# Where the scaled down-projection weights and a residual correction stand in GpSimd's queue

## The chip, the cores and the metric

The kernel runs on one core of a Trainium2 chip. The core has five engines that run side by side, each with its own queue that is worked off in order: PE (TensorE, matrix products), DVE (VectorE), ACT (ScalarE), POOL (GpSimd) and SP (SyncE, which here only issues DMA transfers). They wait for one another through semaphores. The metric is the device time of one execution in microseconds (us), taken as the median of several runs; lower is better. One of those executions is recorded by the hardware profiler, and all durations below are from that record.

## What is computed

One decoder block on a 1024 x 1024 float32 activation: a state-space branch and an attention branch, merged by gates, and a feed-forward network. The change lies in the feed-forward network, of which the reference says:

```python
h = modulate(rmsnorm(x, norm2_g[l]), sh2, sc2)
ffn = (jax.nn.silu(h @ w_ffn_gate[l]) * (h @ w_ffn_up[l])) @ w_ffn_down[l]
x = x + g2 * ffn
...
return rmsnorm(x, norm_f_g)
```

`h` is 1024 x 1024, the hidden width is 2816, and `g2` is a row of 1024 gates. The kernel multiplies the rows of `w_ffn_down` by `g2` instead of the product, so the down projection adds straight to the residual `x`.

## The kernel before

**Pairs.** The hidden width is cut into 11 pieces of 256 columns, called pairs. Piece 10 is computed plainly. Pairs 0 to 9 go through `gate_up`, one after the other, each as a block scheme of seven products for gate and up instead of eight (`ORDER` gives the order of the seven). For every one of the seven, `operand` (L462) forms a weight block: where two blocks have to be added, POOL adds them into a staging tile (L471); ACT makes the rounded high part (L473), DVE the low part (L474). Each product is three matmuls per slice (high by high, high by low, low by high), 12 matmuls for gate and 12 for up, into one PSUM bank each. There are 8 banks, so the fifth product of a pair can only start when the banks of the first are free again.

**Emptying the banks.** `combine` (L1280) adds the seven products into four tiles `f1`: the first product is copied by ACT (L1284), the third too (L1288), the others are added by DVE (L1286 to L1299). Pool `F` holds four buffers of `f1`, all of which a pair uses, so a pair's first copy L1284 has to wait until a buffer of the pair before is free.

**End of a pair.** ACT applies silu to the two gate tiles (L1261), DVE multiplies by up (L1262), and POOL forms five sums of quarters (L1268), called *the pair's sums* below: three into new places, two in place. Then SP issues four DMA writes of the four tiles to `hD` in device memory (L1271). Only when these writes have landed are the `f1` buffers free for the next pair's L1284 and L1288.

**Rows of the down projection.** The down projection runs in three steps (`STEPS` = 4, 3 and 3 pairs), again as seven products. For the first step the right-hand operands are prepared beside `gate_up`: a row block `ft` of `w_ffn_down` is loaded by SP (L1194), multiplied by `g2` on POOL (L1195, *scaling*), and every second pair `down_sums` takes two scaled blocks, lets SP write two quarters to `hD` as they are (L1306), forms five quarter sums on POOL (L1311) in three groups that share one tile `gf`, and has each group written to `hD` (L1313). `ft` has two buffers, `gf` one.

**Start of the down projection.** `down` loads the residual into `acc`, scales the weights of the later steps on POOL (L1340), and corrects one quarter of the residual by two others with four POOL operations on 128 x 1024 (L1363, *the correction*). Its operand tiles partly live in the same `f1` buffers.

**What sets the order.** In this part no order is written by hand. A planner simulates the engines and puts each instruction in its engine's queue, the earliest in the program first among those that are ready in its simulation. `after(ins, first)` (L502) adds an edge that only orders: `ins` is placed behind `first` by the planner, and where the two are on different engines the chip waits for nothing on that account. Once placed, the queues are fixed; on the chip an instruction that is not ready holds up everything behind it on its engine.

Of the kernel before, what the change touches and what calls it, by code (L numbers as in the profile page):

```python
# [9 lines left out]
F32 = mybir.dt.float32  # L10
# [3 lines left out]
ALU = mybir.AluOpType  # L14
# [346 lines left out]
P = 128  # L361
# [25 lines left out]
SIGN_B = {i: ALU.subtract if i in (3, 4) else ALU.add for i in range(1, 8)}  # L387
# [38 lines left out]
class Block:  # L426
# [754 lines left out]
    def ffn(self, const, tp):  # L1181
        nc, i = self.nc, self.i
        wv = [i[n][0].rearrange("(k p) n -> p k n", p=P) for n in ("w_ffn_gate", "w_ffn_up")]
        w_v = i["w_ffn_down"][0].rearrange("(m p) n -> m p n", p=P)
        rows = []
        self.plain(10, wv)
        for j in range(10):
            self.gate_up(j, wv, tp)
            if j == 0:
                g2 = self.rp.tile([P, 1024], F32, name="row")  # L1190
                self.ada_row(g2, 6, tp, self.banks, ("ft", None))
            elif j <= 2 * STEPS[0]:
                rows.append(tp.tile([P, 1024], F32, name="ft"))
                nc.sync.dma_start(out=rows[-1], in_=w_v[j - 1])  # L1194
                nc.gpsimd.tensor_tensor(rows[-1], rows[-1], g2, ALU.mult)  # L1195
                if j % 2 == 0:
                    self.down_sums(j // 2 - 1, rows[-2:], tp)
        self.exp_ln(*self.silus)
        self.down(const, tp, g2)

# [33 lines left out]
    def gate_up(self, pair, wv, tp):  # L1234

        nc = self.nc
        A = {}
        for x, y in ((1, 0), (1, 1), (0, 0), (0, 1)):
            t = A[x, y] = self.W.tile([P, 2, 4, P], F32, name="wb")
            for q in range(2):  # L1240
                nc.sync.dma_start(out=t[:, q], in_=wv[q][:, 4 * y:4 * y + 4, 256 * pair + P * x:256 * pair + P * x + P])
        C = [[self.F.tile([P, 1024], F32, name="f1") for _ in range(2)] for _ in range(2)]
        M = [{}, {}]
        flat = lambda t: t.rearrange("p q k n -> p (q k n)")
        for n, i in enumerate(ORDER):
            if i not in self.B:
                b11, b12, b21, b22 = self.blocks
                u, v, pool, tag = {4: (b21, b11, self.PA, "pa"), 3: (b12, b22, self.PB, "pb"), 1: (b11, b22, self.X, "x1"),
                                   6: (b11, b12, self.X, "x1"), 7: (b21, b22, self.F, "f0")}[i]
                self.B[i] = self.pieces(i, u, v, pool, tag, Turns((tp, "ft")))  # L1250
            a, b = TERMS_A[i]
            w = self.operand(flat(A[a]), b and flat(A[b]), SIGN_A[i], None, *(nc.vector if pair == 0 or (i, e) in AENG else nc.gpsimd for e in range(2)))
            w = [t.rearrange("p (q k n) -> p q k n", q=2, k=4) for t in w]
            for q in range(2):
                ps = M[q][i] = self.banks.tile([P, 512], F32)
                self.seven(ps, w, q, i)
                self.combine(i, M[q], [C[q][0][:, 0:512], C[q][0][:, 512:1024], C[q][1][:, 0:512], C[q][1][:, 512:1024]])
        self.silus = []
        for x in range(2):
            g, u = C[0][x], C[1][x]  # L1260
            self.silus.append(nc.scalar.activation(g, g, AF.Silu))  # L1261
            nc.vector.tensor_tensor(u, u, g, ALU.mult)  # L1262
        L, R = slice(0, 512), slice(512, 1024)
        (g0, g1), (u0, u1) = C
        a11, a12, a21, a22 = u0[:, L], u1[:, L], u0[:, R], u1[:, R]
        for o, a, b, op in ((g0[:, L], a11, a22, ALU.add), (g0[:, R], a21, a22, ALU.add), (g1[:, L], a11, a12, ALU.add),
                                           (a21, a21, a11, ALU.subtract), (a12, a12, a22, ALU.subtract)):
            nc.gpsimd.tensor_tensor(o, a, b, op)  # L1268
        for n, t in ((0, u0), (2, u1), (4, g0), (6, g1[:, L])):
            w = t.shape[-1] // 512  # L1270
            nc.sync.dma_start(out=self.hD[pair, :, n:n + w, 0], in_=t.rearrange("p (a b) -> p a b", a=w))  # L1271
# [26 lines left out]
        elif i == 7:  # L1298
            tt(c[0], m[7], c[0], ALU.add)  # L1299

    def down_sums(self, pair, rows, tp):

        nc = self.nc
        part = lambda ax: rows[ax[0]][:, 512 * ax[1]:512 * ax[1] + 512]
        for i in (2, 5):
            nc.sync.dma_start(out=self.hD[pair, :, SLOT[i], 1], in_=part(TERMS_B[i][0]))  # L1306
        for group in ((3, 6), (7, 4), (1,)):
            t = tp.tile([P, 2, 512], F32, name="gf", bufs=1)
            for n, i in enumerate(group):
                a, b = TERMS_B[i]  # L1310
                nc.gpsimd.tensor_tensor(t[:, n], part(a), part(b), SIGN_B[i])  # L1311
            s = SLOT[group[0]]
            nc.sync.dma_start(out=self.hD[pair, :, s:s + len(group), 1], in_=t[:, 0:len(group)])  # L1313

    def down(self, const, tp, g2):
# [36 lines left out]
        for s, np_ in enumerate(STEPS):  # L1352
            W = [(weights(2 * p), weights(2 * p + 1)) if s else None for p in range(p0, p0 + np_)]
            if s == 1:
                gf = tp.tile([P, 1024], F32, name="gf", bufs=1)
                nc.scalar.dma_start(out=gf, in_=self.i["norm_f_g"].partition_broadcast(P))
            if s == len(STEPS) - 1:
                WL = [weights(20 + m) for m in range(2)]
            for n, i in enumerate(ORDER if s else FIRST):
                if s == 0 and n == 2:  # L1360
                    for z, op in ((5, ALU.add), (4, ALU.subtract)):
                        for a in range(2):
                            nc.gpsimd.tensor_tensor(flat(acc[7][a]), flat(acc[7][a]), flat(acc[z][a]), op)  # L1363
                ops = []
                (ay, ax), b = TERMS_B[i]
                for p in range(np_):
                    st = stages.tile([P, 1024], F32)
                    h, l = tiles()
                    if s == 0:
                        nc.sync.dma_start(out=st.rearrange("p (a b) -> p a b", a=2), in_=self.hD[p, :, SLOT[i]])  # L1370
                        self.operand(st, tiles=(h, l))
                        ops.append((h, l))
                        continue
                    nc.sync.dma_start(out=st[:, L], in_=self.hD[p0 + p, :, SLOT[i], 0])
                    u = W[p][ay][:, 512 * ax:512 * ax + 512]
                    if b is None:
                        for q, v in ((L, st[:, L]), (R, u)):
                            nc.scalar.copy(h[:, q], v)
                            nc.vector.tensor_tensor(l[:, q], v, h[:, q].bitcast(F32), ALU.subtract)
                    else:  # L1380
                        last_sum = nc.gpsimd.tensor_tensor(st[:, R], u, W[p][b[0]][:, 512 * b[1]:512 * b[1] + 512], SIGN_B[i])  # L1381
                        nc.scalar.copy(h, st)
                        nc.vector.tensor_tensor(l, st, h.bitcast(F32), ALU.subtract)
                    ops.append((h, l))
                if s == len(STEPS) - 1:
                    if n == 6:
                        rest = []
                        for m in range(2):
                            st = self.W.tile([P, 1024], F32, name="wb", bufs=4)
                            nc.sync.dma_start(out=st, in_=self.lD[m])  # L1390
                            rest.append((self.operand(st, tiles=tiles()), self.operand(WL[m], tiles=tiles())))
                    closing(n)
                for t in range(4):
                    ps = self.banks.tile([P, 512], F32)
                    j = 0
                    for o in ops:
                        for x, y in PRODUCTS:
                            nc.tensor.matmul(ps, lhsT=o[x][:, P * t:P * t + P], rhs=o[y][:, R], start=(j == 0), stop=(j == 3 * np_ - 1))  # L1398
                            j += 1
                    m = {z: acc[z][t // 2][:, t % 2] for z in acc}  # L1400
                    if s == 0 and i not in FROM:
                        (nc.scalar.copy if (n * 4 + t) % 2 else nc.vector.tensor_copy)(m[i], ps)
                    else:
                        nc.vector.tensor_tensor(m[i], ps, m[i], ALU.add)
            p0 += np_
# [176 lines left out]
```

## Time and profile before

| | us |
|---|---|
| median of 3 runs | 1488.67 |
| lowest and highest | 1486.19, 1491.62 |
| the profiled execution, its own time | 1486.86 |
| its span, first to last instruction | 1485.1 |

The span holds the input projection, the two branches and the output projection up to some 819 us, piece 10 and pairs 0 to 9 from there to 1250 us, and then the down projection with the last norm. In the timelines below a row gives start, duration, engine, line, operation, destination and sources, how many were merged, and in brackets how long the engine had been idle before and what ended that.

### The profile page before, as it was taken

To read this page: it belongs to the slowest core of one execution; us is meant where nothing else is said; L and a number is where in the kernel's file an instruction comes from. 1 tells how busy PE (TensorE), PEld (TensorE's weight loads), DVE (VectorE), ACT (ScalarE), POOL (GpSimd) and SP (SyncE) were. 2 spreads that over 40 slices of the span, in tenths; PEclk is the share of its full clock that TensorE was granted. 3 is DMA by queue.
4 is the path that set the end of the run, shared out by engine and by line. 5 is a ranking of instruction groups with operands and counts; after the bars stand their busy time and mean duration, and the time that the engine had idled before them with its cause. 6 is when DMAs were issued, how large, how long until landed. Compare 5 with 4: busy or idle time off the path is not lost.

```text
span 1485.1 us, 18288 instructions
## 1 busy us (share of the span) xinstructions
PE 1417.7 (95%) x6730; PEld 1121.3 (76%) x6730; DVE 1100.0 (74%) x1436; ACT 633.9 (43%) x859; POOL 497.4 (33%) x265
## 2 busy tenths in 40 slices
PE   5898999999999999999999999898999999999996
PEld 3678888787666666658887788787888888788884
DVE  5779996357797989877715598776756667879997
ACT  3321122632587767773339343222323334443425
POOL 1000000101211112104300017888644449328796
PEclk9999999999999999999999999999999999999998
DMA  9555665479111012126533134545433339745312
GB/s 341 136 112 166 159 166 133 148 251 353 35 50 50 29 43 78 51 76 236 180 118 128 43 86 149 186 164 181 150 101 99 104 105 359 240 130 175 100 57 114
DMA packets 186042, 207.19 MB, mean 140 GB/s; under 512 B 28892, under 2 KB 128288, under 8 KB 185952
## 3 DMA queue, kind: packets, MB, share of 16 engines
q1 hardware_dynamic: 176816, 198.49, 41.9%
q10 hardware_dynamic: 8912, 7.48, 1.8%
q8 instruction: 53, 0.87, 0.2%
q14 instruction: 37, 0.30, 0.1%
q0 software_dynamic: 224, 0.05, 0.0%
HBM read 148.69 MB, written 56.10 MB: 138 GB/s over the span
## 4 chain that ended last, share of the span: by engine, by line
PE 61%; DVE 14%; issue 7%; DMA 6%; POOL 6%; ACT 5%; SPq 0%; DVEq 0%; POOLq 0%; ACTq 0%
PE tq L1277 10%; PE mx L812 5%; PE mm L1277 5%; PE wo L1277 5%; PE ga L738 4%; PE mm L812 4%; PE mm L738 3%; PE acc L812 2%; PE mm L1117 2%; PE mm L646 2%; PE mx L738 2%; PE z L812 2%; PE wo L1117 2%; PE tq L1226 2%; PE tq L1117 1%
## 5 line engine op out<-in xcount | busy, mean ns | idle before, releaser
L471 POOL TENSOR_TENSOR ws<-wb 128x1024 f32<-128x1024 f32 x24 | 61.6, 2567 | 184.2 <-DVE wl L474 162.1
L455 POOL TENSOR_TENSOR wl<-ws,wh 128x1024 fp32r<-128x1024 f32 x12 | 30.7, 2562 | 162.7 <-ACT wh L452 99.3
L905 DVE TENSOR_TENSOR wa<-wa,acc 128x512 f32<-128x512 f32 (+1 forms) x80 | 47.0, 628 | 32.6 <-ACT row L903 30.2
L294 POOL MEMSET tz<- 128x1024 f32 x4 | 3.8, 954 | 178.0 <-PE mm L646 96.0
L877 ACT ACTIVATE ws<-wa 128x1024 f32<-128x1024 f32 (+1 forms) x40 | 39.1, 976 | 48.5 <-DVE wa L874 48.2
L1268 POOL TENSOR_TENSOR f<-f,f 128x512 f32<-128x512 f32 x30 | 53.2, 1800 | 16.0 <-DVE f L1262 10.7
L882 DVE TENSOR_TENSOR wl<-ws,wh 128x1024 fp32r<-128x1024 f32 (+1 forms) x40 | 57.1, 1427 | 1.0
L982 DVE SCALAR_TENSOR_TENSOR acc<-aw,cond,acc 128x512 f32<-128x512 f32 x56 | 46.0, 821 | 6.8 <-DMA aw<-in_w_ada_dram 6.1
L1261 ACT ACTIVATE f<-f 128x1024 f32<-128x1024 f32 x20 | 21.2, 1062 | 67.4 <-DVE f L1297 39.6
L474 DVE TENSOR_TENSOR wl<-ws,wh 128x1024 fp32r<-128x1024 f32 x20 | 33.7, 1683 | 19.7 <-ACT wh L473 19.6
L880 DVE SCALAR_TENSOR_TENSOR ws<-wa,ws 128x1024 f32<-128x1024 f32 (+1 forms) x40 | 45.5, 1137 | 3.0 <-ACT ws L879 2.0
L1398 PE MATMUL tq<-f,f 128*128 128x512 f32 x156 | 47.2, 389 | 0.0
L908 ACT ACTIVATE wa<-wa 128x1024 f32<-128x1024 f32 (+1 forms) x40 | 38.8, 971 | 19.5 <-DVE wa L905 18.5
L452 ACT CAST wh<-ws 128x1024 fp32r<-128x1024 f32 x24 | 25.1, 1049 | 49.8 <-PE wo L1117 23.3
L812 PE MATMUL z<-q,k 64*128 64x512 f32 (+3 forms) x192 | 41.8, 526 | 3.6 <-DVE wa L874 2.4
L471 POOL TENSOR_TENSOR wgs<-wb 128x1024 f32<-128x1024 f32 x12 | 30.8, 2570 | 41.2 <-DVE wgl L474 14.9
L1277 PE MATMUL tq<-x,wh 128*128 128x512 f32 x144 | 44.3, 389 | 0.0
L1277 PE MATMUL tq<-pa,wh 128*128 128x512 f32 x144 | 44.3, 389 | 0.0
L1340 POOL TENSOR_TENSOR pa<-pa,row 128x1024 f32<-128x1024 f32 x14 | 42.0, 3038 | 0.0
L454 POOL TENSOR_SCALAR wh<-ws 128x1024 fp32r<-128x1024 f32 x6 | 7.7, 1277 | 102.3 <-issue 36.1
L1381 POOL TENSOR_TENSOR wb<-pa 128x512 f32<-128x512 f32 x14 | 23.1, 1655 | 55.9 <-DVE wl L474 37.9
L812 PE MATMUL mm<-wa,V 128*64 128x512 f32 (+3 forms) x192 | 39.8, 507 | 0.0
(948 smaller groups left out, 4751.8 us busy)
## 6 DMA issues: line engine op xcount, KB each, us to landing
aw<-in_w_ada_dram SPq DMA_DIRECT2D x64, 256.0 KB, 4.5
hD<-f SPq DMA_DIRECT2D x30, 512.0 KB, 4.0
ws<-in_w_in_dram SPq DMA_DIRECT2D x23, 512.0 KB, 4.3
wb<-in_w_ffn_gate_dram SPq DMA_DIRECT2D x44, 256.0 KB, 4.0
wb<-in_w_ffn_up_dram SPq DMA_DIRECT2D x44, 256.0 KB, 4.5
x<-in_x_dram SPq DMA_DIRECT2D x16, 512.0 KB, 7.1
pb<-in_w_ada_dram SPq DMA_DIRECT2D x16, 512.0 KB, 9.4
gD<-gst SPq DMA_DIRECT2D x32, 256.0 KB, 2.1
```

The source lines that it names most:

```text
L471: (add or nc.gpsimd).tensor_tensor(st, a, b, op)
L738: self.nc.tensor.matmul(ps, lhsT=w[a][:, k], rhs=act[h][k][:, b], start=(j == 0), stop=(j == n - 1))
L812: return self.tc.keep_in_program_order(self.nc.tensor.matmul(*args, **kw))
L880: nc.vector.scalar_tensor_tensor(st, a, 0.0, st, ALU.max, ALU.add)
L882: nc.vector.tensor_tensor(lt, st, ht.bitcast(F32), ALU.subtract)
L905: nc.vector.tensor_tensor(a[:, x, 0:f], a[:, x, 0:f], r[:, x, 0:f], ALU.subtract)
L982: nc.vector.scalar_tensor_tensor(acc, w[:, j], cj, acc, ALU.mult, ALU.add)
L1117: self.nc.tensor.matmul(ps, lhsT=mg[t // 4][k][:, a, P * (t % 4):P * (t % 4) + P], rhs=ws[k // 2][b][:, k % 2], start=k + j == 0, stop=k + ...
L1268: nc.gpsimd.tensor_tensor(o, a, b, op)
L1277: self.nc.tensor.matmul(ps, lhsT=w[x][:, q, k], rhs=self.B[i](y, k), start=(j == 0), stop=(j == 11))
L1340: nc.gpsimd.tensor_tensor(w, w, g2, ALU.mult)
L1398: nc.tensor.matmul(ps, lhsT=o[x][:, P * t:P * t + P], rhs=o[y][:, R], start=(j == 0), stop=(j == 3 * np_ - 1))
```

## The change

Three edits:

1. In `ffn`, the two row blocks for the first step's pair p are loaded and scaled together in loop turn j = 2p + 1 (turns 1, 3, 5, 7) instead of one each in turns 2p + 1 and 2p + 2. Both scalings are ordered behind the second silu of turn j - 1.
2. In `down_sums`, called in the same turn, the first group of quarter sums is ordered behind that same silu, and the second and third groups behind the second silu of turn j.
3. In `down`, the four operations of the correction are ordered behind the last of pair 9's sums (`self.last_sum`).

No operation is added or dropped, and no size is changed.

```diff
-        rows = []
...
             if j == 0:
                 g2 = self.rp.tile([P, 1024], F32, name="row")
                 self.ada_row(g2, 6, tp, self.banks, ("ft", None))
-            elif j <= 2 * STEPS[0]:
-                rows.append(tp.tile([P, 1024], F32, name="ft"))
-                nc.sync.dma_start(out=rows[-1], in_=w_v[j - 1])
-                nc.gpsimd.tensor_tensor(rows[-1], rows[-1], g2, ALU.mult)
-                if j % 2 == 0:
-                    self.down_sums(j // 2 - 1, rows[-2:], tp)
+            elif j % 2 and j < 2 * STEPS[0]:
+                rows = [tp.tile([P, 1024], F32, name="ft") for _ in range(2)]
+                for n, t in enumerate(rows):
+                    nc.sync.dma_start(out=t, in_=w_v[j - 1 + n])
+                    self.after(nc.gpsimd.tensor_tensor(t, t, g2, ALU.mult), silu)
+                self.down_sums(j // 2, rows, tp, (silu, self.silus[-1], self.silus[-1]))
+            silu = self.silus[-1]
...
-            nc.gpsimd.tensor_tensor(o, a, b, op)
+            self.last_sum = nc.gpsimd.tensor_tensor(o, a, b, op)
...
-    def down_sums(self, pair, rows, tp):
+    def down_sums(self, pair, rows, tp, firsts):
...
-        for group in ((3, 6), (7, 4), (1,)):
+        for group, first in zip(((3, 6), (7, 4), (1,)), firsts):
             t = tp.tile([P, 2, 512], F32, name="gf", bufs=1)
             for n, i in enumerate(group):
                 a, b = TERMS_B[i]
-                nc.gpsimd.tensor_tensor(t[:, n], part(a), part(b), SIGN_B[i])
+                self.after(nc.gpsimd.tensor_tensor(t[:, n], part(a), part(b), SIGN_B[i]), first)
...
                     for z, op in ((5, ALU.add), (4, ALU.subtract)):
                         for a in range(2):
-                            nc.gpsimd.tensor_tensor(flat(acc[7][a]), flat(acc[7][a]), flat(acc[z][a]), op)
+                            self.after(nc.gpsimd.tensor_tensor(flat(acc[7][a]), flat(acc[7][a]), flat(acc[z][a]), op), self.last_sum)
```

## The prediction

> **What bounds the kernel now.** I began with the page: its head and the line of busy shares.
>
> ```profile
> span 1485.1 us, 18288 instructions
> PE 1417.7 (95%) x6730; PEld 1121.3 (76%) x6730; DVE 1100.0 (74%) x1436; ACT 633.9 (43%) x859; POOL 497.4 (33%) x265
> ```
>
> PE is the engine that is nearly always busy, so POOL work costs time only where it makes PE stop. The view of waits, for PE from 880 us to the end, lists every stop in the part that the change touches:
>
> ```profile
> engine line waited for: us in total, times, longest us
> PE tq L1277 <- ACT f L1284: 5.5, 1, 5.5
> PE mm L1277 <- ACT f L1284: 4.1, 1, 4.1
> PE mm L1398 <- DVE wgl L474: 1.4, 1, 1.4
> PE tq L1398 <- ACT f L473: 1.0, 2, 0.8
> ```
>
> Four entries, 12 us. The first two belong to `gate_up`, the last two to the start of `down`. The view of windows, cut at the borders of the pairs as PE sees them, shows what they cost (length, then busy time and matmuls of PE, PEld, DVE, ACT and POOL, then granted clock and DMA):
>
> ```profile
> 897.70:936.18 38.48, 38.48 (x171) 31.87 (x170) 32.12 (x29) 10.41 (x13) 33.69 (x16) 1.00 0.45 147
> 936.18:980.10 43.92, 39.78 (x169) 32.44 (x168) 34.45 (x28) 13.07 (x15) 36.67 (x19) 0.96 0.56 190
> 980.10:1026.50 46.40, 40.87 (x168) 33.24 (x167) 28.45 (x27) 10.27 (x12) 41.70 (x22) 0.93 0.53 183
> 1102.68:1140.76 38.08, 38.08 (x170) 31.53 (x169) 23.58 (x26) 11.64 (x13) 18.78 (x10) 1.00 0.33 104
> ```
>
> A pair has 7 x 24 = 168 matmuls and needs 38.08 us when nothing stops (last row), 5.44 per product. The second and third stretch take 43.92 and 46.40, so 5.84 and 8.32 more: **14.16 us** lost. Of that 4.1 and 5.5 are the stops and the other 4.5 is the clock, granted at 0.96 and 0.93 over these stretches instead of 1.00 (43.92 x 0.04 + 46.40 x 0.07 = 5.0).
>
> Why does L1284 come late there? The timeline of POOL at these two pairs, and a pair on time as the last row:
>
> ```profile
> 941.14 5.73 POOL L1195 TENSOR_TENSOR ft<-ft,row 128x1024 f32<-128x1024 f32 x2 [4.57 <-DMA ft<-in_w_ffn_down_dram]
> 946.84 3.38 POOL L471 TENSOR_TENSOR wgs<-wb 128x1024 f32<-128x1024 f32 x1
> 950.17 3.53 POOL L1311 TENSOR_TENSOR gf<-ft 128x512 f32<-128x512 f32 x2
> 953.66 5.72 POOL L1268 TENSOR_TENSOR f<-f,f 128x512 f32<-128x512 f32 x3
> ...
> 988.87 2.84 POOL L1311 TENSOR_TENSOR gf<-ft 128x512 f32<-128x512 f32 x2 [2.90 <-DMA hD<-gf]
> 991.68 2.38 POOL L471 TENSOR_TENSOR ws<-wb 128x1024 f32<-128x1024 f32 x1
> 994.65 1.29 POOL L1311 TENSOR_TENSOR gf<-ft 128x512 f32<-128x512 f32 x1 [0.58 <-DMA hD<-gf]
> 995.90 4.76 POOL L1268 TENSOR_TENSOR f<-f,f 128x512 f32<-128x512 f32 x3
> ...
> 1105.20 4.70 POOL L1268 TENSOR_TENSOR f<-f,f 128x512 f32<-128x512 f32 x3 [1.91 <-DVE f L1262]
> ```
>
> and of DVE and ACT, what makes the sums ready and what waits for them:
>
> ```profile
> 941.23 3.39 DVE L1262 TENSOR_TENSOR f<-f,f 128x1024 f32<-128x1024 f32 x1 [0.53 <-ACT f L1261]
> 985.30 1.75 DVE L1262 TENSOR_TENSOR f<-f,f 128x1024 f32<-128x1024 f32 x1 [0.53 <-ACT f L1261]
> 1099.60 1.22 DVE L474 TENSOR_TENSOR wl<-ws,wh 128x1024 fp32r<-128x1024 f32 x1
> 1103.90 1.23 DVE L1262 TENSOR_TENSOR f<-f,f 128x1024 f32<-128x1024 f32 x1
> 1111.02 2.20 DVE L471 TENSOR_TENSOR wgs<-wb 128x1024 f32<-128x1024 f32 x1
> ```
>
> ```profile
> 961.44 0.59 ACT L1284 COPY f<-mm 128x512 f32<-128x512 f32 x1 [13.16 <-DMA hD<-f]
> 1006.94 0.59 ACT L1284 COPY f<-tq 128x512 f32<-128x512 f32 x1 [14.83 <-DMA hD<-f]
> 1101.45 1.06 ACT L1261 ACTIVATE f<-f 128x1024 f32<-128x1024 f32 x1 [2.91 <-DVE f L1299]
> 1113.35 0.59 ACT L1284 COPY f<-mm 128x512 f32<-128x512 f32 x1 [3.91 <-DMA hD<-f]
> ```
>
> In the undisturbed pair that PE begins at 1102.68 the sums start 2.5 us after its begin and L1284 ends at 1113.94. PE can go on for four products, to 1102.68 + 4 x 5.44 = 1124.44, before it needs that bank. **The margin is 10.5 us.** In the pair begun at 936.18 L1284 ends at 962.03 against a limit of 957.94: 4.1 too late, which is the stop. In that begun at 980.10 it ends at 1007.53 against 1001.86: 5.7, and the trace has 5.5. The sums were ready when L1262 ended, at 944.62 and 987.05, and started at 953.66 and 995.90. So 9.0 and 8.9 us went to row work and one addition (L471) that the planner had put ahead of them, among them waits for a DMA.
>
> **The change, part by part.** It adds and drops no instruction. What it moves, by source line, with minimum, median and maximum in ns:
>
> ```profile
> L1195 POOL TENSOR_TENSOR ft<-ft,row x8: 2338/2412/3393, 907.7 to 1006.5; 128x1024 f32<-128x1024 f32 x8
> L1311 POOL TENSOR_TENSOR gf<-ft x20: 1278/1292/2292, 921.2 to 1023.9; 128x512 f32<-128x512 f32 x20
> ```
>
> and two rows of the queues that the moved steps pass, SP's and ACT's:
>
> ```profile
> 986.00 6.11 SPq L1313 DMA_DIRECT2D hD<-gf  x2
> ```
>
> ```profile
> 1029.03 1.05 ACT L473 CAST wxh<-ws 128x1024 fp32r<-128x1024 f32 x1 [5.68 <-DMA hD<-gf]
> ```
>
> *Rows.* 8 scalings and 20 quarter sums, at the medians 8 x 2.41 + 20 x 1.29 = 45 us of POOL, now lie within the 119 us from 907 to 1026. Bound to turns 1, 3, 5 and 7 they are spread over eight pairs: behind silu 0, 2, 4 and 6 two scalings and two sums (7.4 us), behind silu 1, 3, 5 and 7 three sums (3.9 us). At silu 1 and 2, where the two stops arise, nothing may precede that silu any more.
>
> What can still precede the pair's sums? The planner can only use the gap between the end of the silu and of L1262: 1102.51 to 1105.13, 2.6 us. One scaling fits, or two quarter sums. Beside POOL work L1262 took 3.39 instead of 1.23. The bounds for the lateness: none; or all four operations at once, 5.73 + 3.53 = 9.3, with the slower L1262 11.5 (at the borders with three sums, 3 x 1.76, a wait of 2.90 for `gf` and the same 2.2: 10.4). I take one scaling at its slow 3.4 plus 2.2, 5.6 us, since the gap holds no more; it is under 10.5, so PE doesn't stop. **Both losses go: -14.2.**
>
> What hides the moved work in its new places: an undisturbed pair has 18.78 of 38.08 us on POOL, so at most 18.8 + 9.3 = 28.1 with the slow durations. The pair from 897.70 already carries 33.69 of POOL, two scalings and five quarter sums among it, and PE loses nothing there. On SP each row pair moves two loads, two writes of quarters and three of groups; a write that waits for its sums holds the weight loads behind it. At 986 two such writes held the queue for 6.1 us, and PE's waits list no load. ACT's queue has the load of the norm's row into `gf`, which waits for the last group; that goes along to the pair behind silu 7. It held ACT for 5.7 us here and cost nothing, being under the margin. Each I cost at 0; if the cover goes, the price is that of the second rival.
>
> *Correction.* The start of `down`, POOL first, then DVE, ACT and PE:
>
> ```profile
> 1251.09 13.20 POOL L1363 TENSOR_TENSOR pb<-pb 128x1024 f32<-128x1024 f32 x4 [0.62 <-issue]
> 1264.25 6.74 POOL L1268 TENSOR_TENSOR f<-f,f 128x512 f32<-128x512 f32 x3
> 1270.95 4.60 POOL L1268 TENSOR_TENSOR f<-f 128x512 f32<-128x512 f32 x2
> ```
>
> ```profile
> 1259.39 2.65 DVE L1262 TENSOR_TENSOR f<-f,f 128x1024 f32<-128x1024 f32 x1
> 1261.97 3.41 DVE L474 TENSOR_TENSOR wgl<-wb,wgh 128x1024 fp32r<-128x1024 f32 x1
> 1306.45 0.68 DVE L1404 TENSOR_TENSOR pb<-mm,pb 128x512 f32<-128x512 f32 x1
> ```
>
> ```profile
> 1279.04 1.04 ACT L473 CAST f<-wgs 128x1024 fp32r<-128x1024 f32 x1 [5.19 <-DMA hD<-f]
> ```
>
> The last sums are ready at 1262.04 and wait 2.2 us for the correction; while it runs, DVE is slow (L474 3.41 for 1.22). Behind the sums the correction ends by 1262.0 + 11.3 + 13.2 = 1286.5, and its result is read at 1306.45, 20 us later, so waiting costs nothing there. ACT's cast at 1279.04 waits for the sums' writes and makes PE stop for 1.0; that should go, as the sums come 2.2 us earlier or more. The 1.4 behind the slow L474 may go, or appear again beside the correction in its new place. Bounds: 2.4 gained, or as much lost; I take half the stops, **-1.2**, as the release of the tiles is certain and the rest open.
>
> Sum: 1486.86 - 14.2 - 1.2 = 1471.5 for the profiled execution. It lay 1.8 below the median of the three runs, so against that median the forecast is **1473.3 us** (-1.0%).
>
> **The rivals.**
>
> *One of the two stops stays.* The planner's time isn't the chip's; if it still puts a scaling, a sum and an L471 ahead of one pair's sums, the larger loss may remain: 1473.3 + 8.3 = 1481.6. For it: the planner misjudged both pairs. Against: nothing older than the silu can stand there. 0.12.
>
> *Slower: sums behind a row that hasn't landed.* If both scalings come ahead of the sums in POOL's queue and their load isn't there, POOL stands still with everything behind. Price: wait 4.6 (as at 941.14) + 9.3 + 2.2 = 16.1 us late, 5.6 over the margin, which cost 8.32 in the pair from 980.10; at four borders 33.3: 1506.6. With all four operations ahead it outweighs the gain from a wait of about 1.1 us up: then each border stops PE for 2.1 and loses 1.7 of clock, 15 us in all. Against: the `ft` buffers are free again nearly a pair earlier, so the load has some 30 us. 0.08.
>
> *DVE and POOL get in each other's way.* L474 took 1.22 alone, L1262 3.39 instead of 1.23 beside POOL. If the two engines' two-input operations only took turns, an undisturbed pair would hold 7 x 1.22 + 2.20 + 2 x 1.23 = 13.2 on DVE and 18.8 on POOL, and the four loaded ones 7.4 more: 39.4 for 38.08. That is 1.3 us too much, and with a loss of clock as in the first stop (5.84 - 4.1 = 1.7) 3.0 in each of four pairs: 1473.3 + 12 = 1485.3. Against: the pair between has 35.9, which pays it back, and 10.5 of margin lie ahead. 0.08. The Trainium skill, "SBUF — State Buffer", section "SBUF: two separate sides", speaks for this rival: it calls the port pair that both engines use an exclusive lock, held for a whole instruction, where the other blocks. By that rule the times add as here; the trace's slowed operations agree with it, though no row of this case shows who held the port.
>
> *The change does nothing:* the queues come out much as they were, 1488.7. The traces of the planner's order speak against it, since silu 1 and 2 lie behind much of the row work. 0.04.
>
> **How the numbers follow.** The forecast has 0.68. A measurement of this kernel tells 0.3%, about 4.5 us, from no change. Faster: the forecast and the first rival, 0.80; within 0.3%: the third and fourth, 0.12; slower: 0.08. The range takes in the forecast, with both bounds of the correction and the runs' spread, and the first rival with 2 us to spare: 1468.5 to 1484.
>
> **What would show it.** Right: no PE wait for L1284 left; the pairs at 38.1 us each with clock 1.00 from 897 to 1250; the rows' scalings in four clusters some 76 us apart; sums within 6 us of L1262's end; the correction behind 1262. Wrong: a PE stop at L1284 in a pair with scalings, a POOL wait for `ft` ahead of the sums, a new stop between 1260 and 1310 longer than 2.4 us, or PE stops behind L474 in loaded pairs.

## The result and the profile after

| | us |
|---|---|
| before, median of 8 runs | 1487.3 (1483.7 to 1492.38) |
| changed, median of 8 runs | 1477.46 (1470.05 to 1481.03) |
| ratio of the two, 95% interval | 0.9928 [0.9903, 0.9954] |
| profiled execution of the changed kernel, its own time | 1480.38 |

The changed kernel is faster by 0.7%. The forecast was 1473.3 us, in a range of 1468.5 to 1484. One later run of the kernel before took 1587.66 us at a granted clock of 0.845, and the ratios in this document leave it out. The head of the changed kernel's page, and its view of waits for PE from 880 us to the end:

```profile
span 1478.7 us, 18286 instructions
PE 1416.4 (96%) x6730; PEld 1121.6 (76%) x6730; DVE 1097.4 (74%) x1436; ACT 634.0 (43%) x859; POOL 496.2 (34%) x265
```

```profile
engine line waited for: us in total, times, longest us
PE tq L1398 <- DVE f L474: 3.2, 1, 3.2
```

Where four stops stood there is one. Both stops at L1284 are gone, and so are the 1.4 and 1.0 at the start of the down projection; a stop of 3.2 us is new. The windows of the pairs that had lost time, and of the two behind them, cut again some 0.3 us ahead of PE's begin of each pair (same columns as before):

```profile
943.60:981.70 38.10, 38.10 (x170) 31.55 (x169) 31.06 (x28) 12.07 (x14) 30.08 (x14) 1.00 0.50 167
981.70:1019.80 38.10, 38.10 (x169) 31.55 (x169) 29.40 (x28) 12.49 (x14) 26.60 (x14) 1.00 0.41 132
1019.80:1057.90 38.10, 38.10 (x169) 31.54 (x169) 26.15 (x26) 10.74 (x13) 28.10 (x15) 1.00 0.48 160
1057.90:1096.00 38.10, 38.10 (x169) 31.53 (x168) 24.84 (x26) 12.53 (x14) 22.45 (x12) 1.00 0.38 123
```

The first two are the pairs that took 43.92 and 46.40 us; both take 38.10 now, at clock 1.00. In the last two POOL is busy for 28.1 and 22.5 us where it was 20.6 and 18.8, and PE doesn't notice.

To see where the time went I compare the same instructions of both traces: the first and the last matmul of one frequent group in the pairs, and the last one of the last product (by source line: minimum, median, maximum in ns, then first and last start). Before, then after:

```profile
L1277 PE MATMUL tq<-x,wh x144: 389/389/389, 883.4 to 1249.3; 128*128 128x512 f32 x144
L1435 PE MATMUL tq<-f,f x24: 389/389/395, 1448.9 to 1470.2; 128*128 128x512 f32 x24
```

```profile
L1277 PE MATMUL tq<-x,wh x144: 389/389/500, 891.0 to 1242.7; 128*128 128x512 f32 x144
L1435 PE MATMUL tq<-f,f x24: 389/389/395, 1442.5 to 1463.7; 128*128 128x512 f32 x24
```

| part | before | after | |
|---|---|---|---|
| ahead of the group's first matmul | 883.4 | 891.0 | +7.6 |
| pairs, first to last of the group | 365.9 | 351.7 | -14.2 |
| from there to the last product's end | 220.9 | 221.0 | +0.1 |

The pairs won 14.2 us. The start of the down projection won nothing. And the profiled execution of the changed kernel began its pairs 7.6 us later, though every engine has the same instructions in the same order up to there; over all twelve profiles of this study the pairs' group begins between 883.1 and 891.0 us. That is why the two profiled executions differ by 6.5 us only. 5.0 of the 7.6 us arose in one stretch, which begins with the same matmul in both kernels and ends where the pairs' matmuls begin. Its windows, before and after:

```profile
267.40:858.90 591.50, 579.46 (x2611) 428.26 (x2611) 414.39 (x473) 345.65 (x454) 85.98 (x48) 0.99 0.34 114
270.00:866.50 596.50, 583.82 (x2612) 431.81 (x2611) 413.32 (x473) 345.76 (x455) 86.03 (x48) 0.98 0.34 113
```

The granted clock was 0.99 and 0.98, and PE was busy for 4.4 us longer on the same work. So most of that part is the clock; what lowers it there isn't shown.

### The profile page after: what moved, and what is told of

It is laid out like the page before. It is cut to its first block, busy times and chain, and to the rows that moved or that the text cites. A ratio compares the mean times of both kernels' runs of the same rounds, so it can differ in the third digit from the quotient of the medians.

```text
span 1478.7 us, 18286 instructions
## 1 busy us (share of the span) xinstructions
PE 1416.4 (96%) x6730; PEld 1121.6 (76%) x6730; DVE 1097.4 (74%) x1436; ACT 634.0 (43%) x859; POOL 496.2 (34%) x265
## 4 chain that ended last, share of the span: by engine, by line
PE 64%; DVE 16%; issue 7%; ACT 5%; DMA 5%; POOL 2%; SPq 0%; DVEq 0%; POOLq 0%; ACTq 0%
PE tq L1277 13%; PE wo L1277 6%; PE mm L1277 6%; PE mx L812 5%; PE mm L812 4%; PE ga L738 4%; PE acc L812 2%; PE mm L1117 2%; PE mm L646 2%; DMA aw<-in_w_ada_dram 2%; PE z L812 2%; PE tq L1226 2%; PE wo L1117 2%; PE mm L738 2%; PE tq L1117 1%
## 5 line engine op out<-in xcount | busy, mean ns | idle before, releaser
L982 DVE SCALAR_TENSOR_TENSOR acc<-aw,cond,acc 128x512 f32<-128x512 f32 x56 | 41.8, 746 | 8.6 <-DMA aw<-in_w_ada_dram 8.0
L452 ACT CAST wh<-ws 128x1024 fp32r<-128x1024 f32 x24 | 25.1, 1049 | 52.9 <-PE wo L1117 26.4
L473 ACT CAST wh<-ws 128x1024 fp32r<-128x1024 f32 x20 | 21.1, 1053 | 47.1 <-PE tq L1277 27.6
```

The source lines that it names most:

```text
L982: nc.vector.scalar_tensor_tensor(acc, w[:, j], cj, acc, ALU.mult, ALU.add)
```

## The experiments

In the table below "pairs" is the length of the group above, "down" what follows to the last product, and "stops" are PE's waits at the copy L1284 and at the start of `down`. Ratios come from runs beside the kernel before. Where there was one run only, its time in us stands in place of a ratio; the kernel before beside these took 1483.65, also in one run.

| kernel | pairs | down | stops L1284 | stops down | ratio |
|---|---|---|---|---|---|
| before | 365.9 | 220.9 | 4.1 + 5.5 | 1.4 + 1.0 | |
| before, second profile | 365.8 | 221.0 | 3.6 + 6.3 | 1.4 + 1.4 | 0.9998 [0.9985, 1.0012] |
| changed | 351.7 | 221.0 | none | 3.2 | 0.9928 [0.9903, 0.9954] |
| changed, again | 351.4 | 222.6 | none | 3.2 | 0.9932 [0.9910, 0.9954] |
| rows only | 351.4 | 220.4 | none | 1.2 + 0.4 | 0.9929 [0.9914, 0.9944] |
| correction only | 366.0 | 222.5 | 3.1 + 6.4 | 3.2 | one run, 1492.69 |
| no order edges | 366.2 | 220.5 | 3.8 + 6.7 | 1.4 + 0.5 | one run, 1488.92 |
| real waits | 351.7 | 221.0 | none | 3.2 | one run, 1477.80 |
| correction on DVE | 351.4 | 217.5 | none | none | 0.9895 [0.9881, 0.9909] |
| correction on DVE, again | 351.4 | 217.4 | none | none | 0.9885 [0.9867, 0.9904] |
| half the correction deferred | 351.6 | 217.5 | none | none | 0.9908 [0.9895, 0.9921] |

**The changed kernel again, and before again.**

> The changed kernel once more, to tell its worth from the scatter of the part ahead of the pairs. My theory: the first to the last matmul of the row tq<-x,wh of L1277 take 351.7 us again (365.9 before), from there to the last matmul of the last product 221 (220.9 before), and the begin of the pairs scatters by several us between executions of either kernel. Then the ratio is 0.988 to 0.993. Rival: the new order costs something ahead of the pairs too; then its pairs again begin some 7 us later than those of before in this profile, and the ratio stays at 0.993 or above.

> The kernel before once more, for a second profile of it: the timings of the changed kernels lie 2 to 4 us above what their traces give against the one profile of before. Theory: the part ahead of the pairs scatters by some 7 us in every kernel, and before's first profile had a short one (pairs from 883.4; the seven others of changed kernels 884 to 891); then its pairs begin at 885 to 890 here, and the pairs themselves take 366 us again. Rival: the changed kernels are slower ahead of the pairs; then they begin at 883 to 884 here again. Second rival: before's two stops are not always that long; then its pairs take less than 364 here.

The parts repeat to within 0.3 us in the pairs, and before's two stops with them. The ratio of the changed kernel, 0.9932, lies on the border between theory and rival. The begin of the pairs was 885.3 in the changed kernel and 883.1 in before, so the second expectation missed here: it had 885 to 890, and 883.1 is what its rival named, that the changed kernels are slower ahead of the pairs. Against that rival stand the kernel with extra additions on POOL (below), which is the kernel before up to pair 4 and whose group began at 887.9, and two changed kernels: rows only began at 884.1 and the correction on DVE at 883.7. Scatter is the likelier reading, but both profiles of before have the two shortest times, and twelve profiles don't settle whether that is chance. The 1.6 us between the two profiles of the changed kernel behind the pairs are the clock. The windows of the 63 us behind the pairs, first of the first profile, then of the second:

```profile
1242.70:1306.00 63.30, 60.10 (x265) 49.43 (x264) 50.99 (x41) 29.10 (x33) 23.66 (x10) 1.00 0.71 242
```

```profile
1236.70:1300.00 63.30, 60.10 (x258) 49.32 (x257) 50.60 (x40) 27.82 (x31) 23.70 (x10) 0.97 0.72 242
```

Both have the stop of 3.2; in one execution the clock stayed at 1.00, in the other it fell to 0.97 of the stretch (0.03 x 63.3 = 1.9 us). So the same stop cost 3.2 or some 5 us. Two more kernels have this stop, and over the same 63.3 us from the end of the group the clock was 1.00 with the real waits and 0.97 with the correction only.

**Rows only, correction only.** The edit of the first takes the third edit back, that of the second takes the third edit alone:

```diff
-    self.after(nc.gpsimd.tensor_tensor(flat(acc[7][a]), flat(acc[7][a]), flat(acc[z][a]), op), self.last_sum)
+    nc.gpsimd.tensor_tensor(flat(acc[7][a]), flat(acc[7][a]), flat(acc[z][a]), op)
```

> Edits 1 and 2 alone, the correction left where it was. My theory: the whole gain is the two stops at L1284, so the pairs take 351.7 us as with the whole change, the stops of 1.4 and 1.0 us at the start of the down projection are back and the one of 3.2 is gone, and the time is that of the whole change to within 1 us. Rival: the correction's place carries a part of the gain; then this is slower than the whole change by 2 us or more.

> Edit 3 alone on the kernel before. My theory: the two stops at L1284 are there as before (4.1 and 5.5 us, pairs 365.9 us), and the start of the down projection looks as with the whole change: no stop of 1.4 or 1.0, one of about 3.2 us. No difference of the time that can be measured.

PE's waits in the kernel with the rows only, and in the one with the correction only:

```profile
PE mm L1398 <- DVE wgl L474: 1.2, 1, 1.2
PE tq L1398 <- ACT f L473: 0.4, 1, 0.4
```

```profile
PE tq L1277 <- ACT f L1284: 6.4, 1, 6.4
PE tq L1398 <- DVE f L474: 3.2, 1, 3.2
PE mm L1277 <- ACT f L1284: 3.1, 1, 3.1
```

Edits 1 and 2 bring the whole gain of the pairs, 14.5 us (365.9 - 351.4). Edit 3 is worth nothing: beside rows only, the whole change takes 0.6 us more behind the pairs (221.0 - 220.4), or 2.2 when the clock falls behind the stop (222.6). In the timings rows only (0.9929) and the whole change (0.9932, beside the same runs of before) can't be told apart.

**No order edges.** The loads and scalings in pairs, as in the change, but every `after` on the row work and on the correction taken away:

```diff
-    self.after(nc.gpsimd.tensor_tensor(t, t, g2, ALU.mult), silu)
+    nc.gpsimd.tensor_tensor(t, t, g2, ALU.mult)
...
-    self.after(nc.gpsimd.tensor_tensor(t[:, n], part(a), part(b), SIGN_B[i]), first)
+    nc.gpsimd.tensor_tensor(t[:, n], part(a), part(b), SIGN_B[i])
...
-    self.after(nc.gpsimd.tensor_tensor(flat(acc[7][a]), flat(acc[7][a]), flat(acc[z][a]), op), self.last_sum)
+    nc.gpsimd.tensor_tensor(flat(acc[7][a]), flat(acc[7][a]), flat(acc[z][a]), op)
```

> The two row blocks are loaded and scaled together in turns 1, 3, 5 and 7 as in the change, but without any order edge. POOL's queue is then in the same order of kinds as before the change. My theory: the order on POOL is what counts, so both stops at L1284 are there, 4 to 6 us each, and the pairs take 364 to 368 us. Rival: bringing the loads together in the program is enough; then 352 us.

Both stops are back (3.8 and 6.7) and the pairs take 366.2; at these two pairs the sums start 9.0 and 8.9 us behind L1262's end, as in the kernel before. Loading the rows together does nothing by itself; what the change is worth lies in the places that the edges give the row work in POOL's queue.

**Doses of POOL work ahead of the sums.** In the kernel before, in pairs 4 to 7, where nothing else stands there:

```diff
+    for _ in range({4: 3, 5: 5, 6: 8, 7: 11}.get(pair, 0)):
+        wait = nc.gpsimd.tensor_tensor(g1[:, R], u1[:, L], u1[:, R], ALU.add)
     for o, a, b, op in ((g0[:, L], a11, a22, ALU.add), (g0[:, R], a21, a22, ALU.add), (g1[:, L], a11, a12, ALU.add),
                                        (a21, a21, a11, ALU.subtract), (a12, a12, a22, ALU.subtract)):
-        nc.gpsimd.tensor_tensor(o, a, b, op)
+        s = nc.gpsimd.tensor_tensor(o, a, b, op)
+        if 4 <= pair <= 7:
+            self.after(s, wait)
```

> The kernel before, with extra additions on POOL (128 x 512, into a place that nobody reads, waiting for L1262) ahead of the sums of pairs 4, 5, 6 and 7: 3, 5, 8 and 11 of them, no DMA. My theory: only the lateness of the sums against L1262's end counts, and PE stops by that lateness less 10.5 us. At an estimated 1.2 to 2.2 us each: pair 4 4 to 7 us late and pair 5 6 to 11, no stop or under 1; pair 6 10 to 18, a stop of 0 to 7; pair 7 13 to 24, a stop of 3 to 13, each with 1.7 to 3.4 of lower clock. Rival: the stops come from the DMA queue (rows and their writes ahead of the sums' writes); then there is no stop in these pairs, as no DMA is added.

POOL and ACT at the two strongest doses, and PE's waits from 1040 to 1260 us (the lines stand four further down in this kernel: L1270 are the sums, L1288 is the copy L1284):

```profile
1160.94 3.77 POOL L1270 TENSOR_TENSOR f<-f,f 128x512 f32<-128x512 f32 x3
...
1205.88 3.70 POOL L1270 TENSOR_TENSOR f<-f,f 128x512 f32<-128x512 f32 x3
```

```profile
1166.39 0.59 ACT L1288 COPY f<-tq 128x512 f32<-128x512 f32 x1 [8.77 <-DMA hD<-f]
...
1211.27 1.22 ACT L1288 COPY f<-tq 128x512 f32<-128x512 f32 x2 [10.15 <-DMA hD<-f]
```

```profile
PE tq L1281 <- ACT f L1288: 6.3, 1, 6.3
```

The begin of each following pair on PE is found by counting 168 matmuls per pair; the limit is that begin plus 21.76 us, four products:

| extra additions | sums behind L1262's end | first copy ends | limit | PE stops |
|---|---|---|---|---|
| 3 | 3.3 | 1083.85 | 1091.23 | no |
| 5 | 7.0 | 1124.00 | 1129.32 | no |
| 8 | 12.8 | 1166.97 | 1167.39 | no |
| 11 | 17.7 | 1211.85 | 1205.47 | 6.3 |

POOL's lateness alone, without a single DMA more, makes the stop, and its size is the copy's end less the limit (6.38 worked out, 6.3 in the view). The pair with the stop took 46.40 us at a granted clock of 0.93:

```profile
1183.70:1230.10 46.40, 40.13 (x169) 32.75 (x168) 28.01 (x27) 12.68 (x14) 35.64 (x20) 0.93 0.27 85
```

These are the length and the clock of the pair with before's second stop; the rest of the 8.3 us lost, 2.0, is the lower clock. The rule "lateness less 10.5 us" gives 2.3 and 7.2 us for the two strongest doses, measured were none and 6.3. So DMA traffic isn't needed for a stop. It isn't out of the picture either, and the margin is no constant 10.5 us: here 12.8 us passed with 0.4 to spare, because the copy began 5.5 us behind the sums (1160.94 to 1166.39). In the undisturbed pair of before that took 8.2 us, and at before's second stop 11.0 (995.90 to 1006.94), while its row loads and writes shared the DMA engines. The window of that moment in the kernel before:

```profile
1000.00:1006.00 6.00, 2.05 (x10) 1.35 (x8) 1.75 (x1) 0.00 (x0) 5.89 (x4) 1.00 1.06 388
```

The last two numbers are the DMA engines' busy share, over 1, and 388 GB/s. The 2.9 us between the two (11.04 - 8.15) are a part of that stop; most of them lie between the issue of the first write and the copy. That the row traffic is the reason is argued and not shown, as the last section says.

**Real waits in place of order edges.**

```diff
+    def behind(self, ins, first):
+        self.tc.add_manual_dep(ins.ins, first.ins.name, mybir.DependencyInfo(mybir.DependencyClass.Sync, mybir.DependencyReason.DATA), reason="order")
...
-    self.after(nc.gpsimd.tensor_tensor(t, t, g2, ALU.mult), silu)
+    self.behind(nc.gpsimd.tensor_tensor(t, t, g2, ALU.mult), silu)
...
-    self.after(nc.gpsimd.tensor_tensor(t[:, n], part(a), part(b), SIGN_B[i]), first)
+    self.behind(nc.gpsimd.tensor_tensor(t[:, n], part(a), part(b), SIGN_B[i]), first)
```

> The whole change with real waits (semaphores) in place of the order edges on the scalings and quarter sums. With edges that only order, POOL did the row work ahead of the silu named, in time that it would have idled. My theory: with real waits it starts only behind the silu, still ahead of the sums in the queue, so that the sums come 8 to 12 us after L1262 at the pairs with scalings and 5 to 9 at the others: at the margin of 10.5, so stops at L1284 of 0 to 3 us at up to four pairs, 0 to 15 us in all. Rival: the real wait changes nothing, because POOL reaches that work after the silu anyway; then 351.7 us for the pairs.

ACT, then POOL, at the pair whose sums follow the second two scalings (L1266 is the silu, L1200 the scaling, L1273 the sums):

```profile
975.10 1.06 ACT L1266 ACTIVATE f<-f 128x1024 f32<-128x1024 f32 x1 [5.54 <-DVE f L1302]
981.40 1.06 ACT L1266 ACTIVATE f<-f 128x1024 f32<-128x1024 f32 x1 [4.30 <-DVE f L1304]
```

```profile
976.24 6.79 POOL L1200 TENSOR_TENSOR ft<-ft,row 128x1024 f32<-128x1024 f32 x2 [2.85 <-ACT f L1266]
...
990.81 4.76 POOL L1273 TENSOR_TENSOR f<-f,f 128x512 f32<-128x512 f32 x3
```

The waits are real now (2.85 us here), and the sums come 6.7 us behind L1262's end at 984.11, yet there is no stop: the pairs take 351.7. I had expected 8 to 12 at the pairs with scalings and up to four stops. The reason is that the silu named by the edge is the earlier of the two, which these rows show: the scalings start with its end at 976.16, not with that of the other at 982.46. It came close: the first copy that follows ended at 999.86 for a limit of 1001.14, and one pair earlier at 962.71 for 963.06.

**The new stop at the start of the down projection.** Two kernels take POOL's correction away from the splits there. One puts it on DVE, without an edge; the other keeps it on POOL and lets one of its four operations wait for the last copy of the second product:

```diff
-    self.after(nc.gpsimd.tensor_tensor(flat(acc[7][a]), flat(acc[7][a]), flat(acc[z][a]), op), self.last_sum)
+    nc.vector.tensor_tensor(flat(acc[7][a]), flat(acc[7][a]), flat(acc[z][a]), op)
```

```diff
+    c = nc.gpsimd.tensor_tensor(flat(acc[7][a]), flat(acc[7][a]), flat(acc[z][a]), op)
+    self.after(c, self.last_sum)
+    if z == 5 and a == 0:
+        self.behind(c, copied)
```

> Edits 1 and 2, and the correction on DVE instead of POOL (same four operations, no order edge). My theory of the new 3.2 us stop: DVE's splits L474 take 3.4 us instead of 1.2 beside the correction on POOL, and PE waits for one of them. With the correction on DVE four operations of about 1.3 us are added there, but the splits run at 1.2 and the stop at 1276 goes: 1 to 3 us faster than the whole change. Rival: the stop is the load of the operands from hD; then it stays, and DVE is only busier.

> The whole change, with the correction's first operation really waiting (a semaphore, not an order edge alone) for the last copy of the second product of the down projection. My theory: the splits between 1262 and 1275 run at 1.2 us and the 3.2 us stop goes; the correction then ends some 13 us after that copy, close to where its result is read, so a stop of up to 3 us may come there instead. Rival (load of the operands): the 3.2 us stop stays.

> Edits 1 and 2 with the correction on DVE once more. Theory: pairs 351.4 us and the part behind them 217.5 to its last product again, no PE stop behind 880 us, ratio 0.988 to 0.991.

First the changed kernel, POOL, DVE and PE at the stop:

```profile
1251.54 5.76 POOL L1268 TENSOR_TENSOR f<-f,f 128x512 f32<-128x512 f32 x3 [7.77 <-issue]
...
1261.73 12.40 POOL L1363 TENSOR_TENSOR pb<-pb 128x1024 f32<-128x1024 f32 x4
```

```profile
1265.13 3.42 DVE L474 TENSOR_TENSOR f<-wgs,f 128x1024 fp32r<-128x1024 f32 x1
1268.48 3.41 DVE L474 TENSOR_TENSOR wxl<-ws,wxh 128x1024 fp32r<-128x1024 f32 x1
1271.81 3.41 DVE L474 TENSOR_TENSOR f<-ws,f 128x1024 fp32r<-128x1024 f32 x1
1275.14 1.21 DVE L474 TENSOR_TENSOR f<-wb,f 128x1024 fp32r<-128x1024 f32 x1
```

```profile
1276.40 0.96 PE L1398 MATMUL tq<-f,f 128*128 128x512 f32 x3 [3.20 <-DVE f L474]
```

While the correction runs, each of these splits takes 3.4 us; the moment it ends, at 1274.13, the next takes 1.21, and that is the one PE waits for. In the kernel with the correction on DVE, DVE has it at 1.2 us an operation in time when POOL idles:

```profile
1239.73 2.35 DVE L1363 TENSOR_TENSOR pb<-pb 128x1024 f32<-128x1024 f32 x2
...
1243.14 1.22 DVE L1363 TENSOR_TENSOR pb<-pb 128x1024 f32<-128x1024 f32 x1
...
1244.87 1.22 DVE L1363 TENSOR_TENSOR pb<-pb 128x1024 f32<-128x1024 f32 x1
```

No stop is left behind 880 us, the part behind the pairs takes 217.5 instead of 221.0, and the ratio is 0.9895 and 0.9885: **faster than the kernel before and than the changed one** (0.9932 [0.9910, 0.9954] beside the first). I had expected 1 to 3 us over the whole change; behind the pairs it is 3.5. In the other kernel the planner put two of the four operations ahead of the one that waits, so only half was deferred:

```profile
1257.89 5.75 POOL L1368 TENSOR_TENSOR pb<-pb 128x1024 f32<-128x1024 f32 x2
1271.86 6.17 POOL L1368 TENSOR_TENSOR pb<-pb 128x1024 f32<-128x1024 f32 x2 [8.22 <-DMA ws<-hD]
```

```profile
1261.28 3.44 DVE L474 TENSOR_TENSOR f<-wgs,f 128x1024 fp32r<-128x1024 f32 x1
1264.64 1.21 DVE L474 TENSOR_TENSOR wxl<-ws,wxh 128x1024 fp32r<-128x1024 f32 x1
```

That was enough: between the two halves the splits run at 1.21, and PE doesn't stop. The rival of the late load falls: the loads read what the sums' writes leave, and the sums come no earlier in these two kernels, 14.6 us behind the end of the pairs' group with the correction on DVE (1249.73 - 1235.1) and 8.9 with half of it deferred (1247.70 - 1238.8), against 8.8 in the changed kernel. The Trainium skill, "SBUF — State Buffer", section "SBUF: two separate sides", has the two engines share one port pair by an exclusive lock; 3.4 beside POOL and 1.2 without agrees with that, but the traces show the durations only, not who held a port.

## Why the prediction was right, and where it was not

**The two stops.** Right in size and place. They were to give 14.2 us, and the pairs went from 365.9 to 351.7. That the row work ahead of the sums causes them was argued from before's rows and is now shown: without the edges they return, and POOL work alone makes such a stop. The account of how it does so had two steps wrong, which follow.

**What stands ahead of the sums.** The step "The planner can only use the gap between the end of the silu and of L1262: 1102.51 to 1105.13, 2.6 us. One scaling fits, or two quarter sums." was wrong, though its result held. POOL and ACT of the changed kernel:

```profile
974.12 5.75 POOL L1195 TENSOR_TENSOR ft<-ft,row 128x1024 f32<-128x1024 f32 x2
979.83 4.51 POOL L1311 TENSOR_TENSOR gf<-ft 128x512 f32<-128x512 f32 x2
984.31 2.40 POOL L471 TENSOR_TENSOR ws<-wb 128x1024 f32<-128x1024 f32 x1
987.87 6.67 POOL L1268 TENSOR_TENSOR f<-f,f 128x512 f32<-128x512 f32 x3 [1.17 <-DVE f L1262]
```

```profile
962.90 0.59 ACT L1284 COPY f<-mm 128x512 f32<-128x512 f32 x1 [6.73 <-DMA hD<-f]
...
975.88 1.06 ACT L1261 ACTIVATE f<-f 128x1024 f32<-128x1024 f32 x1 [3.70 <-DVE f L1297]
983.83 1.06 ACT L1261 ACTIVATE f<-f 128x1024 f32<-128x1024 f32 x1 [5.94 <-DVE f L1299]
```

All four row operations and an addition stand ahead of the sums, and still the sums start on the heel of L1262. I had taken the silu that ends last, 1102.51. But `silus[-1]` is that of the second tile, which waits for the sixth product (L1297) and comes first on the chip; the seventh (L1299) completes the first tile. Between that earlier silu and L1262 lie 11 us here (976.94 to 987.79), and the whole row work fits. Besides, an order edge doesn't hold POOL: the scalings began at 974.12, before the silu they are "behind". So the lateness was 0.1 us in most pairs and 1.1 in one (5.6 forecast).

**The margin.** 10.5 us was read from one pair as if it belonged to the sums' lateness behind L1262. The prediction's own rows contradict that: in the two pairs that stopped, this lateness was 9.0 and 8.9 us, which is less than 10.5. What it left out is the lateness of L1262 itself. In the undisturbed pair L1262 ended 2.2 us behind PE's begin (1105.13, with the begin at 1102.90 when counted by matmuls); in the two pairs that stopped, 8.6 and 6.9 us behind it (944.62 - 936.02 and 987.05 - 980.13). By these numbers, with the rest left as it was, an L1262 on time would have spared the first stop and left 0.9 us of the second (2.2 + 8.8 + 11.6 - 21.76, an estimate). In the pair of before that follows, L1262 was late too, the sums followed at once, and PE didn't stop:

```profile
1033.14 1.84 DVE L1262 TENSOR_TENSOR f<-f,f 128x1024 f32<-128x1024 f32 x1 [0.53 <-ACT f L1261]
```

```profile
1035.07 6.67 POOL L1268 TENSOR_TENSOR f<-f,f 128x512 f32<-128x512 f32 x3 [1.17 <-DVE f L1262]
```

With PE's begin at 1026.74, L1262 ended 8.2 us behind it, and the first copy ended 4.5 us ahead of the limit. The other way round, sums 12.8 us late behind an L1262 that ended 2.5 us after PE's begin passed as well (the dose of 8). The change took away the sums' lateness; L1262 is still late in these two pairs, 6.0 and 5.8 us behind the begins at 943.91 and 981.99:

```profile
948.10 1.84 DVE L1262 TENSOR_TENSOR f<-f,f 128x1024 f32<-128x1024 f32 x1 [0.53 <-ACT f L1261]
...
984.92 2.87 DVE L1262 TENSOR_TENSOR f<-f,f 128x1024 f32<-128x1024 f32 x1 [0.53 <-ACT f L1261]
```

Why it is late there no run shows. The limit itself, four products behind PE's begin, held at every pair of the four kernels in which it was worked out; the time from the sums' begin to the copy's end varied from 6.0 to 13.0 us. At the copy of 962.90 of the changed kernel it was 12.4, and only 2.2 us were left to the limit. With the forecast lateness of 5.6 us in place of 1.1 that copy would have ended some 2.3 us past it (5.6 - 1.1 - 2.2, an estimate that leaves the rest as it was). So it was partly luck that both losses went: the lateness and the margin were both smaller than reckoned.

**The cover.** Costs of 0 for SP, ACT and POOL in the later pairs were right: 28.1 us of POOL had been forecast as the most, the windows from 943.60 and 1019.80 have 30.08 and 28.10, and PE lost nothing in either. The two rivals of rows that haven't landed and of a full port in the pairs didn't come.

**The correction.** Forecast -1.2, measured +0.1 and +1.7 against before's 220.9. The term had the right parts, but was put together wrongly. The release came, earlier than reckoned: counted from the end of the pairs' group the sums began 8.8 us behind it (1251.54 - 1242.7) instead of 15.0 (1264.25 - 1249.3). The last L1262 took 1.23 us instead of 2.65 and ended 8.7 us behind the group's end instead of 12.7, and the wait of 2.2 us for the correction was gone. That release was not needed, though: with the correction on DVE the sums came as late as before (14.6) and PE didn't stop. What was left open, the slow splits "beside the correction in its new place", ate it all with a 3.2 us stop at 1276. The prediction had named a new stop between 1260 and 1310 of more than 2.4 us as a sign of being wrong, and for this term it was. The mechanism of the third rival was the one that acted here, not in the pairs.

**The total.** The median came out at 1477.46 us for a forecast of 1473.3. The parts of the traces give -14.2 + 0.1 or -14.5 + 1.7, so -14.1 or -12.8; the timings of the changed kernel give -10.7 (0.0072 x 1487.3) with -6.8 and -14.4 as ends. The forecast of -15.4 was thus too large by the correction's term. The rest is not in the parts from the pairs on, and it is smaller than the scatter ahead of them, 7.9 us from the earliest to the latest of twelve profiles. A part of it is the clock: a run's span times one minus its granted clock, averaged, is 26.1 us in the 11 runs of before that stand beside the changed kernel's second set of runs, 24.6 in those 6 runs, and 22.7 in its first 8. By this estimate 1.5 to 3.4 us of lost clock came back, where the two pairs alone had lost 5.0 (43.92 x 0.04 + 46.40 x 0.07). What lowers the clock elsewhere, and what causes the remaining scatter, stays open.

## What to carry to other kernels

An engine that is a third busy can still stop the one that bounds, if its queue holds postponable work ahead of the one result that frees a buffer; look for the end of the wait, then for what stood ahead in that queue, and move that, not the wait. When work is tied behind an event, check in the trace which instance of the event it is, and whether the tie is a wait or only an order: here the tie named the earlier of two activations, and the work ran ahead even of that. And before moving work on POOL, read what DVE does at the new place: its own durations there (1.2 or 3.4 us for one split) say what the move costs.

## What the runs showed of the hardware that was not expected

The same stop of 3.2 us left the clock at 1.00 in two profiles (the changed kernel, the real waits) and took it to 0.97 of a 63 us stretch in two others (the changed kernel again, the correction only), so a short stop's price varies by about 2 us from run to run.

And sums that began 15.3 us after PE's begin of the pair (8 extra additions; 1160.94 - 1145.63) let PE go on, where sums that began 15.8 us after it had stopped PE for 5.5 us in the kernel before (995.90 - 980.13). The difference lies in the writes. SP's rows for them, in before and then with the 8 extra additions:

```profile
999.67 4.83 SPq L1271 DMA_DIRECT2D hD<-f  x4
```

```profile
1163.50 7.46 SPq L1275 DMA_DIRECT2D hD<-f  x4
```

From there to the first copy passed 7.3 us in before (1006.94) and 2.9 with the additions (1166.39). The DMA engines' busy share was 1.06 from 1000 to 1006 us in the one, and 0.56 from 1163 to 1167 us in the other, so traffic beside the writes is a likely reason. It need not be the rows: in the undisturbed pair the same stretch took 4.7 us, and in the last pair of before, long after the rows, 6.8 with loads of other weights between the writes.
